# Matmuls of the convolution taps, the stick-breaking scores and the state-space outputs contract over 128 partitions instead of 64; the taps' strided operand becomes contiguous

## Chip, cores and metric

One core of one Trainium2 chip. The metric is the device time of one execution, in microseconds, median of three runs.

## The reference

Two blocks of two layers each run over 1024 tokens of width 1024. The first block has a pooling and attention layer and a Hyena layer; the second has a state-space (S5) layer and a stick-breaking attention layer, each followed by a gated feed-forward net. Three places matter here:

```
# Hyena filters: hidden units (64 wide, two sine layers) times w3, 1024 positions
h = (hdn @ w3).reshape(L, HY_ORDER, 2, HY_WIDTH) * decay

# S5 output: states (64 per group) times C, plus a local term and the skip
y = einsum('lbgp,ghp->blgh', s_re, c_re) - einsum('lbgp,ghp->blgh', s_im, c_im) + d_skip * x

# stick-breaking attention, 16 heads of 64
z = einsum('bhqd,bhkd->bhqk', q, k) * 64 ** -0.5
weights = exp(log_sigmoid(z) + (reverse cumulative sum of log_sigmoid(-z)))    # masked to the past
```

## The kernel before, in words

Activations stand transposed (channels on the 128 partitions, tokens along the row). Most products split both operands into a high and a low part of float32r and add three matmuls (`mm3`, lines 202 to 204). Side work is written as generators that `Work.go` advances by a rate per matmul step, so that its instructions stand between the steps of the big products; a tile scheduler then fixes each engine's order. SBUF tiles of 4 KB a partition come from one pool of 40 buffers (`t`, `tr`).

**Taps** (`hy_filters`, `hy_prep`, `hy_spectrum`). The filter taps of 8 x 128 positions are products of the hidden units `hs` with panels of `w3`. `hs` holds the high part of the 64 hidden units on partitions 0 to 63 and the low part on 64 to 127. Line 896 multiplies all 128 rows with `w3h` (its 64 rows stand there twice); line 897 multiplies rows 0 to 63 with `w3l`. The stationary operand is `hsr[:, n + i]`: 128 columns that lie 8 elements apart. There are 12 spectra of 16 such matmuls. Two spectra run in the first 100 us, among the loads of the modulation weights; ten are spread over the products of `ev_in`.

**S5 outputs** (`s5_load`, `outputs` in `s5_main`). Channels come in 8 batches. Of a batch, `s5_load` reads the tables E, ph, D and Co and `u_tile` reads U (eight loads), all on SP's queue. `outputs` computes 8 groups: line 1519 is a 128-row matmul with D; lines 1520 and 1521 contract the real and imaginary states of one group over its 64 partitions (0 to 63 for even groups, 64 to 127 for odd ones). They are plain float32, so the trace shows each as two matmuls.

**Scores** (`sb_q`, `sb_k`, `sb_weights`). For each of 8 pairs of heads, copies on POOL's DMA queue make `q2` (the high part of the queries, on both halves of the partitions) and `k2` (high part of the keys on one half, low part on the other). Line 1926 multiplies them over 128 rows, line 1928 adds the mask, and line 1931 adds low queries times high keys over the 64 rows of the head, `ql[own]` and `k2[e][own]`. A tile of 128 queries has one or two such matmuls, for up to 1024 keys. ScalarE's two sigmoids, a scan on VectorE (line 1940) and a product (line 1942) give the weights, which are transposed (line 1961) and multiplied with the values (lines 1983, 1984). `sb_mix` runs 64 units (pair, head, a quarter of the queries); the scores of the next unit, and the queries, keys and values of the next pair, stand between the products of the current one.

Of the kernel before, what the change touches and what calls it, by code (L numbers as in the profile page):

```python
# [19 lines left out]
P = 128  # L20
# [24 lines left out]
class Work:  # L45
    """instructions that are issued between others, `rate` steps behind each step of a product"""
# [15 lines left out]
class Norm:  # L62
    """layer norm to a (hi, lo) tile per half, and to DRAM; st: the tiles and their sums, set by their product;
    keep: the float32 result replaces the tiles"""
# [39 lines left out]
class Core:  # L104
# [27 lines left out]
    def with_work(self, gen, fg, rate):  # L132
        """runs fg with gen between its products, then the rest of gen"""
        w = Work(gen, rate)
        self.work.insert(0, w)
        fg()
        w.drain()
        self.work.remove(w)

    def lagged(self, tasks):  # L140
        """(product, use) pairs: each use is issued behind the next product"""
# [33 lines left out]
    def weights(self, src, shape, big=False):  # L175
        """a panel of weights as (hi, lo) tiles"""
# [11 lines left out]
    def first4(self, srcs, acts):  # L188
        """four panels, the first half of all before the second; acts: tiles and columns of each half"""
# [55 lines left out]
    def rms_half(self, xs, acc, hv, gain, shift, outs, n=HB):  # L245
        """generator"""
# [19 lines left out]
    def modulation0(self):  # L266
        """shift and scale of block 0, for both conditions"""
# [31 lines left out]
    def mod_cols(self, src, th, b0, out):  # L299
        """1024 columns of a modulation, for the first condition"""  # L300
# [31 lines left out]
    def halves(hs):  # L332
        """tiles and columns of each half of the tokens"""
# [371 lines left out]
    def out_proj(self, wsrc, acts, evac, order=None, first_half=None, res=None):  # L705
        """first_half: Work, issued along with the second half of the tokens; res: tiles and what they start with"""
# [38 lines left out]
    def hy_filters(self):  # L745
        """hidden units of the filters, [64, L]; the halves of L share the partitions until the end"""
# [35 lines left out]
        hl = self.tr("hsl", (P, 2, HB))  # L782
        self.split(src, hl[:, 0], hl[:, 1])
        hs = self.tr("hs", (P, 2, HB))
        for i in range(2):
            for part in range(2):
                nc.gpsimd.dma_start(hs[64 * part:64 * part + 64, i].bitcast(F32),
                                    hl[64 * i:64 * i + 64, part].bitcast(F32))
        self.hs2 = hs.rearrange("p a b -> p (a b)")
# [7 lines left out]
    def cpair(self, out, a, b, sg):  # L797
        """out[0] = a + sg i b, out[1] = a - sg i b"""
# [7 lines left out]
    def dft8(self, x, sg, sl):  # L806
        """8 point transform of complex [4, 2, 128] tiles, in the orders of T2"""
# [43 lines left out]
    def hy_prep(self):  # L851
# [7 lines left out]
        def load(g):  # L859
# [4 lines left out]
            nc.gpsimd.dma_start(w3[0][64:].bitcast(F32), w3[0][:64].bitcast(F32))  # L864
# [17 lines left out]
    def hy_spectrum(self, g, o, ct, w3, dec, skip):  # L882
# [4 lines left out]
        hsr = self.hs2.rearrange("p (a b) -> p b a", b=8)  # L887
# [4 lines left out]
        def taps(n):  # L892
            pb = self.psb("pf")
            for i in range(2):
                ob = pb[:, i * CTX:(i + 1) * CTX]
                mm(ob, hsr[:, n + i], w3[0][:, cs], start=True, stop=False)
                mm(ob, hsr[:64, n + i], w3[1][:64, cs], start=False, stop=True)
# [60 lines left out]
    def modulation1(self):  # L958
        """gate of block 0, shift and scale of block 1, gate of block 1"""
# [21 lines left out]
    def hy_natural(self, c, part, c0):  # L981
        """a panel behind its short convolution, in a frame of 128 positions per partition"""
# [32 lines left out]
    def hy_conv(self, c, y):  # L1015
# [9 lines left out]
        for o in range(2):  # L1025
# [5 lines left out]
            def sums(neg):  # L1031
                """sums (differences) of the transforms of m and m + 4: two in PSUM, two in SBUF"""
# [432 lines left out]
    def s5_load(self, b):  # L1465
        ts = self.s5t[b] = {}
        for n, sh, src in (("E", (P, 8, 2, 64), self.e_d[b]), ("ph", (P, 2, 4, P), self.p_d[b]),
                           ("D", (P, 8, P), self.m_d[b]), ("Co", (P, 2, 4, P), self.c_d[b])):
            ts[n] = self.t("s5" + n, sh)
            self.nc.sync.dma_start(ts[n], src)  # L1470

    def u_tile(self, b):
        """a batch of channels of the S5 layer, eight tokens on the partitions"""
# [6 lines left out]
    def s5_main(self):  # L1480
# [28 lines left out]
        def outputs(b):  # L1509
# [3 lines left out]
            for hb in range(2):  # L1513
                py = self.psb("py5")
                for j in range(4):
                    g = 2 * j + hb
                    o = py[:, j * P:(j + 1) * P]
                    r = slice(hb * 64, hb * 64 + 64)
                    nc.tensor.matmul(o, Dm[:, g], U[:, g], start=True, stop=False)
                    nc.tensor.matmul(o, Co[r, 0, j], S[r, 0, j], start=False, stop=False)  # L1520
                    nc.tensor.matmul(o, Co[r, 1, j], S[r, 1, j], start=False, stop=True)
# [21 lines left out]
        def glu(b):  # L1543
            """the first two panels of the next product grow with the tiles"""
# [81 lines left out]
    def mix_out(self, wsrc, acts, res_d, norm, perm=False):  # L1626
        """out projection + ALPHA * residual (in DRAM), with the sums that the norm needs"""
# [584 lines left out]
```

## Time and profile before

| what | value |
|---|---|
| median of three runs | 4174.78 us (4172.21 to 4179.71) |
| profiled execution, first to last instruction | 4172.6 us |
| busy: PE, VectorE, ScalarE, POOL | 95%, 68%, 35%, 6% |
| granted TensorE clock, mean | 0.964 of full speed |
| chain that ended last | PE 81%, DVE 9%, issue 4%, ACT 3%, DMA 2% |

PE is TensorE's matmuls and PEld its weight loads, which may run beside matmuls. A matmul's listed duration includes its way through the array, so consecutive matmuls overlap; what a matmul costs is the distance between its start and the next start. The page gives no time for the profiled execution besides its span, which is 2.2 us under the median of the runs; what lies around the span is taken to be the same before and after.

### The profile page before, as it was taken

The page shows a single profiled execution, that of the slowest core. Times are in us where ns is not written, and L with a number is a line of the kernel's source. Part 1 is how long each engine was busy: PE and PEld are TensorE (multiplying, and loading weights), DVE is VectorE, ACT ScalarE, POOL GpSimd, SP SyncE. Part 2 cuts the span into 40 slices and gives each one's busy share as a digit, 9 for nine tenths or more (in the row PEclk, how much of TensorE's full clock was granted, in tenths as well). Part 3 has the DMA queues.
Part 4 walks back from the last instruction along what each step waited for, and adds up shares of the span by engine and source line. Part 5 has one row for each costly group of instructions (what it writes and reads, how often), then busy time and mean ns, then how long its engine had stood idle before and what let it go on. Part 6 is the DMA issues. An engine that isn't in the chain of part 4 may idle for free.

```text
span 4172.6 us, 51168 instructions
## 1 busy us (share of the span) xinstructions
PE 3949.0 (95%) x19684; PEld 3206.1 (77%) x19684; DVE 2844.1 (68%) x4892; ACT 1446.3 (35%) x2328; POOL 270.2 (6%) x482
## 2 busy tenths in 40 slices
PE   6899989999999997999999999989999899999997
PEld 3787878777888866787788888768778677888886
DVE  4666667777788968776866664367777867666544
ACT  2222225543121121333433233245555544332332
POOL 0000100022001011000000000010000000000000
PEclk9899999999999998999999999989999899999998
DMA  5333321144122247513322244322222232222542
GB/s 201 107 120 122 116 87 41 36 165 165 66 73 85 74 143 245 174 61 97 131 76 76 91 149 167 108 82 76 61 62 72 75 121 106 76 91 76 174 153 102
DMA packets 169978, 449.16 MB, mean 108 GB/s; under 512 B 37854, under 2 KB 58340, under 8 KB 169734
## 3 DMA queue, kind: packets, MB, share of 16 engines
q1 hardware_dynamic: 129126, 317.94, 23.0%
q0 software_dynamic: 38304, 123.24, 8.5%
q10 hardware_dynamic: 2304, 4.72, 0.4%
q8 instruction: 155, 2.54, 0.2%
q14 instruction: 89, 0.73, 0.1%
HBM read 327.07 MB, written 100.66 MB: 103 GB/s over the span
## 4 chain that ended last, share of the span: by engine, by line
PE 81%; DVE 9%; issue 4%; ACT 3%; DMA 2%; POOL 0%; SPq 0%; ACTq 0%; DVEq 0%; POOLq 0%
PE p L202 7%; PE p L204 7%; PE p L203 7%; PE pd L202 4%; PE pd L204 4%; PE pd L203 4%; PE pout L202 2%; PE pout L204 2%; PE pout L203 2%; DVE sbm L1940 2%; PE pu L202 2%; PE pu L204 2%; PE pu L203 2%; PE pwt L1961 1%; PE pz L1041 1%
## 5 line engine op out<-in xcount | busy, mean ns | idle before, releaser
L185 DVE TENSOR_TENSOR wl<-wt,wh 128x1024 fp32r<-128x1024 f32 x232 | 283.1, 1221 | 335.7 <-ACT wh L184 332.0
L184 ACT CAST wh<-wt 128x1024 fp32r<-128x1024 f32 x232 | 243.0, 1048 | 761.7 <-PE pd L203 213.5
L202 PE MATMUL p<-tq,wq 128*128 128x512 f32 x736 | 292.3, 397 | 3.6 <-ACT wq L215 3.6
L204 PE MATMUL p<-tq,wq 128*128 128x512 f32 x736 | 292.0, 397 | 0.0
L203 PE MATMUL p<-tq,wq 128*128 128x512 f32 x736 | 291.6, 396 | 0.0
L202 PE MATMUL pd<-hd,wh 128*128 128x512 f32 x704 | 278.9, 396 | 0.0
L204 PE MATMUL pd<-hd,wl 128*128 128x512 f32 x704 | 278.7, 396 | 0.0
L203 PE MATMUL pd<-hd,wh 128*128 128x512 f32 x704 | 278.6, 396 | 0.0
L204 PE MATMUL p<-hq,wq 128*128 128x512 f32 x480 | 190.0, 396 | 0.0
L203 PE MATMUL p<-hq,wq 128*128 128x512 f32 x480 | 189.9, 396 | 0.0
L202 PE MATMUL p<-hq,wq 128*128 128x512 f32 x480 | 189.7, 395 | 0.0
L215 ACT CAST wq<-ws 128x512 fp32r<-128x512 f32 x184 | 114.3, 622 | 211.5 <-PE p L204 206.6
L1711 DVE TENSOR_TENSOR fsg<-fsg,p 128x512 f32<-128x512 f32 x140 | 94.3, 686 | 120.1 <-PE p L204 119.9
L202 PEld LDWEIGHTS p<-tq,wq 128*128 128x128 f32 x736 | 138.9, 189 | 43.7 <-ACT wq L215 4.9
L204 PEld LDWEIGHTS p<-tq,wq 128*128 128x128 f32 x736 | 138.8, 189 | 32.4
L203 PEld LDWEIGHTS p<-tq,wq 128*128 128x128 f32 x736 | 139.2, 189 | 31.4
L1711 DVE TENSOR_TENSOR fsu<-fsu,p 128x512 f32<-128x512 f32 x140 | 94.5, 687 | 95.4 <-PE p L204 95.3
L216 DVE TENSOR_TENSOR wq<-ws,wq 128x512 fp32r<-128x512 f32 x184 | 126.6, 689 | 46.8 <-ACT wq L215 44.7
L204 PEld LDWEIGHTS pd<-hd,wl 128*128 128x128 f32 x704 | 132.5, 188 | 31.8
L203 PEld LDWEIGHTS pd<-hd,wh 128*128 128x128 f32 x704 | 132.5, 188 | 31.8
L202 PEld LDWEIGHTS pd<-hd,wh 128*128 128x128 f32 x704 | 132.4, 188 | 31.7
L202 PE MATMUL pu<-hq,wh 128*128 128x512 f32 x320 | 130.0, 406 | 9.4 <-DVE cv L978 9.4
(699 smaller groups left out, 10749.8 us busy)
## 6 DMA issues: line engine op xcount, KB each, us to landing
wt<-w_gu SPq DMA_DIRECT2D x88, 512.0 KB
wt<-w_dn SPq DMA_DIRECT2D x88, 512.0 KB
wm<-w_mod SPq DMA_DIRECT2D x48, 512.0 KB
hid<-fsg POOLq DMA_DIRECT2D x44, 512.0 KB, 4.0
hr<-hid SPq DMA_DIRECT2D x44, 512.0 KB
wt<-w_od SPq DMA_DIRECT2D x28, 512.0 KB
khat<-fX POOLq DMA_DIRECT2D x24, 512.0 KB, 3.0
kh<-khat SPq DMA_DIRECT2D x24, 512.0 KB
```

Source lines behind the costliest of these rows:

```text
L184: nc.scalar.copy(wh, wt)
L185: nc.vector.tensor_tensor(wl, wt, wh.bitcast(F32), op=ALU.subtract)
L202: mm(ps, lh, rh, start=first, stop=False)
L203: mm(ps, lh, rl, start=False, stop=False)
L204: mm(ps, ll, rh, start=False, stop=last)
L215: self.nc.scalar.copy(h, src)
L216: self.nc.vector.tensor_tensor(l, src, h.bitcast(F32), op=ALU.subtract)
L1041: mm(p4[:, i, q], tb[:, m], z[:, self.POS[m]], start=True, stop=False)
L1711: add = lambda o, u, v: tt(o, u, v, op=ALU.add)
L1940: nc.vector.tensor_tensor_scan(om[:, :n - 1], om[:, :n - 1], self.inv[:, 3:4].to_broadcast([P, n - 1]), 1.0, op0=ALU.mult, op1=ALU.add)
L1961: nc.tensor.transpose(pt[:, s * P:(s + 1) * P], W[x][:, c:c + P], self.ident)
```

## The change

`hs8` stores the hidden units in the order in which the taps read them, so that the 128 columns of a load lie next to each other; the copies that build it write rows of 64 elements. `w3l` is copied to partitions 64 to 127 as `w3h` was, and line 897 contracts over 128. In S5, Co comes as two tiles per batch, each with one half loaded and the other set to zero by POOL, and both state products contract over 128 rows. For the scores, four more copies per pair make `l2`, the low queries on both halves, and the matmul contracts over 128 rows of `l2` and `k2`. (The docstrings that the diff also removes change nothing.)

```
@@ hy_filters
-        hl = self.tr("hsl", (P, 2, HB))
-        self.split(src, hl[:, 0], hl[:, 1])
-        hs = self.tr("hs", (P, 2, HB))
+        hl = self.tr("hsl", (P, 2, 8, 64))
+        self.split(src.rearrange("p (a b) -> p a b", b=8), *(hl[:, i].rearrange("p b a -> p a b") for i in range(2)))
+        self.hs8 = self.tr("hs", (P, 8, P))
         for i in range(2):
             for part in range(2):
-                nc.gpsimd.dma_start(hs[64 * part:64 * part + 64, i].bitcast(F32),
+                nc.gpsimd.dma_start(self.hs8[64 * part:64 * part + 64, :, 64 * i:64 * i + 64].bitcast(F32),
                                     hl[64 * i:64 * i + 64, part].bitcast(F32))
-        self.hs2 = hs.rearrange("p a b -> p (a b)")
@@ hy_prep, load
-            nc.gpsimd.dma_start(w3[0][64:].bitcast(F32), w3[0][:64].bitcast(F32))
+            for part in w3:
+                nc.gpsimd.dma_start(part[64:].bitcast(F32), part[:64].bitcast(F32))
@@ hy_spectrum
-        hsr = self.hs2.rearrange("p (a b) -> p b a", b=8)
+        hsr = self.hs8
                 mm(ob, hsr[:, n + i], w3[0][:, cs], start=True, stop=False)
-                mm(ob, hsr[:64, n + i], w3[1][:64, cs], start=False, stop=True)
+                mm(ob, hsr[:, n + i], w3[1][:, cs], start=False, stop=True)
@@ s5_load
-                           ("D", (P, 8, P), self.m_d[b]), ("Co", (P, 2, 4, P), self.c_d[b])):
+                           ("D", (P, 8, P), self.m_d[b])):
+        ts["Co"] = []
+        for hb in range(2):
+            own, oth = slice(64 * hb, 64 * hb + 64), slice(64 - 64 * hb, P - 64 * hb)
+            co = self.t("s5Co", (P, 2, 4, P))
+            self.nc.gpsimd.memset(co[oth], 0.0)
+            self.nc.sync.dma_start(co[own], self.c_d[b][own])
+            ts["Co"].append(co)
@@ s5_main, outputs
-                    nc.tensor.matmul(o, Co[r, 0, j], S[r, 0, j], start=False, stop=False)
-                    nc.tensor.matmul(o, Co[r, 1, j], S[r, 1, j], start=False, stop=True)
+                    nc.tensor.matmul(o, Co[hb][:, 0, j], S[:, 0, j], start=False, stop=False)
+                    nc.tensor.matmul(o, Co[hb][:, 1, j], S[:, 1, j], start=False, stop=True)
@@ sb_q
+        q2, l2 = ([self.tr(n) for _ in range(2)] for n in ("q2", "l2"))
                 nc.gpsimd.dma_start(q2[e][r].bitcast(F32), qh[own].bitcast(F32))
+                nc.gpsimd.dma_start(l2[e][r].bitcast(F32), ql[own].bitcast(F32))
-        yield q2, ql
+        yield q2, l2
@@ sb_weights
-                nc.tensor.matmul(ps[:, c0:c1], ql[own, qc], k2[e][own, ks], start=False, stop=True)
+                nc.tensor.matmul(ps[:, c0:c1], l2[e][:, qc], k2[e][:, ks], start=False, stop=True)
```

On PE the order stays as it was but for the first taps and for the first score tile of the second head of a pair, in seven of the eight pairs. There the scores (`psz`) stood behind the products with the values of the unit before (`pso`). PE before:

```order
L204 MATMUL psg<-hq,wl 128x512
L1983 MATMUL pso<-wT,sbv 128x256
L1984 MATMUL pso<-wT,sbv 128x256
L1983 MATMUL pso<-wT,sbv 128x128
L1984 MATMUL pso<-wT,sbv 128x128
L1926 MATMUL psz<-k_20864,q_20848 128x512
L1928 MATMUL psz<-sbmask,identr 128x128
L1926 MATMUL psz<-k_20864,q_20848 128x512
L1931 MATMUL psz<-k_20864,sql 128x512 x2
```

PE with the change (the same lines are six numbers higher):

```order
L204 MATMUL psg<-hq,wl 128x512
L1932 MATMUL psz<-k_20905,q_20883 128x512
L1934 MATMUL psz<-sbmask,identr 128x128
L1932 MATMUL psz<-k_20905,q_20883 128x512
L1989 MATMUL pso<-wT,sbv 128x256
L1937 MATMUL psz<-k_20905,l_20885 128x512 x2
L1932 MATMUL psz<-k_20905,q_20883 128x512
L1990 MATMUL pso<-wT,sbv 128x256
L1989 MATMUL pso<-wT,sbv 128x256
L1990 MATMUL pso<-wT,sbv 128x256
```

The scores now stand ahead of eight value products, six of 256 columns and two of 128.

POOL's queue issues the copies of a pair's queries (`q`, high part; `l`, low part) and keys (`k`). Of the first pair, before:

```order
L1871 DMA q_20847<-sqh 64x1024 x2
L1871 DMA q_20848<-sqh 64x1024 x2
L1883 DMA k_20863<-skh 64x1024
L1884 DMA k_20863<-skl 64x1024
L1883 DMA k_20864<-skh 64x1024
L1884 DMA k_20864<-skl 64x1024
```

With the change:

```order
L1877 DMA q_20882<-sqh 64x1024
L1878 DMA l_20884<-sql 64x1024
L1877 DMA q_20882<-sqh 64x1024
L1878 DMA l_20884<-sql 64x1024
L1877 DMA q_20883<-sqh 64x1024
L1878 DMA l_20885<-sql 64x1024
L1877 DMA q_20883<-sqh 64x1024
L1878 DMA l_20885<-sql 64x1024
L1890 DMA k_20904<-skh 64x1024
L1891 DMA k_20904<-skl 64x1024
L1890 DMA k_20905<-skh 64x1024
L1891 DMA k_20905<-skl 64x1024
```

The keys' copies have four more copies ahead of them.

## Rows read from the trace of the kernel before

**Rows 1.** The page's first line.

```profile
span 4172.6 us, 51168 instructions
```

**Rows 2.** Busy time by stretch: length, busy of PE to POOL, clock, DMA share, GB/s.

```profile
107.00:530.00 423.00, 407.94 (x1994) 329.41 (x1994) 261.74 (x481) 97.41 (x133) 35.02 (x49) 0.94 0.34 116
1640.00:1730.00 90.00, 82.21 (x546) 64.87 (x542) 70.75 (x142) 18.00 (x22) 4.00 (x12) 0.87 0.83 259
2860.00:3290.00 430.00, 411.99 (x2375) 337.98 (x2373) 340.43 (x435) 233.78 (x434) 27.73 (x54) 0.98 0.24 66
3290.00:3345.00 55.00, 44.35 (x207) 33.74 (x208) 46.74 (x63) 29.86 (x60) 1.09 (x2) 0.77 0.24 83
```

**Rows 3.** Timeline of PE at one group of four taps: start, us, what.

```profile
223.05 0.28 PE L896 MATMUL pf<-w3h,hs 128*128 128x256 f32 x1
223.27 0.51 PE L897 MATMUL pf<-w3l,hs 64*128 64x256 f32 x1
...
224.59 0.50 PE L202 MATMUL pbg<-hh,wh 128*128 128x512 f32 x1
```

**Rows 4.** The chain, in order of time: start, time to the next start, what.

```profile
41.29 0.54 PE pf L896
...
62.41 0.22 PE pk L947 x2
...
2889.90 0.23 PE psg L203
...
2912.56 0.12 PE psv L204
```

**Rows 5.** Weight loads of the taps: ns min/median/max, first and last start.

```profile
L896 PEld LDWEIGHTS pf<-w3h,hs x96: 312/315/335, 36.9 to 526.0; 128*128 128x128 f32 x96
```

**Rows 6.** Weight loads of the scores, the same columns.

```profile
L1926 PEld LDWEIGHTS psz<-k,q x192: 186/189/338, 2787.7 to 3333.4; 128*128 128x128 f32 x192
...
L1931 PEld LDWEIGHTS psz<-k,sql x192: 182/183/335, 2789.1 to 3334.1; 64*128 64x128 f32 x192
```

**Rows 7.** Timeline of PE at one score tile.

```profile
2900.86 0.39 PE L1926 MATMUL psz<-k,q 128*128 128x384 f32 x1
2901.17 0.66 PE L1931 MATMUL psz<-k,sql 64*128 64x512 f32 x2
2901.77 0.50 PE L202 MATMUL psg<-hq,wh 128*128 128x512 f32 x1
2902.11 0.40 PE L203 MATMUL psg<-hq,wh 128*128 128x512 f32 x1
```

**Rows 8.** PE's waits, 2787 to 3345: us in total, times, longest.

```profile
PE pwt L1961 <- DVE sbb L1942: 13.7, 22, 1.6
...
PE psz L1926 <- DMA k<-skl: 5.8, 1, 5.8
```

**Rows 9.** The chain at the first unit of a second head.

```profile
2897.45 0.66 PE psz L1931 x2
...
2906.93 0.30 PE pwt L1961
```

**Rows 10.** Timeline of POOL, copies of the first pair's queries.

```profile
2778.92 2.08 POOL L1871 DMA_DIRECT2D q<-sqh  x4 [26.45 <-ACT sqh L1864]
```

**Rows 11.** Timeline of PE, one group of S5 outputs at full clock, one at half.

```profile
1718.64 0.49 PE L1519 MATMUL py<-s5U,s5D 128*128 128x128 f32 x2
...
1719.70 0.49 PE L1519 MATMUL py<-s5U,s5D 128*128 128x128 f32 x2
...
1757.41 0.79 PE L1519 MATMUL py<-s5U,s5D 128*128 128x128 f32 x2
...
1759.28 0.80 PE L1519 MATMUL py<-s5U,s5D 128*128 128x128 f32 x2
```

**Rows 12.** Timeline of SP, loads of the last batch, and the first matmul on them.

```profile
1719.15 9.26 SPq L1478 DMA_DIRECT2D s5U<-xf_d  x8
...
1730.96 1.09 PE L1492 MATMUL pe_re<-s5U,s5E 128*64 128x128 f32 x16 [1.88 <-DMA s5yt<-s5y]
```

More of the change, by code (lines that the diff above doesn't have):

```diff
@@ L1517, in outputs @@
                     o = py[:, j * P:(j + 1) * P]
-                    r = slice(hb * 64, hb * 64 + 64)
                     nc.tensor.matmul(o, Dm[:, g], U[:, g], start=True, stop=False)
-                    nc.tensor.matmul(o, Co[r, 0, j], S[r, 0, j], start=False, stop=False)
-                    nc.tensor.matmul(o, Co[r, 1, j], S[r, 1, j], start=False, stop=True)
+                    nc.tensor.matmul(o, Co[hb][:, 0, j], S[:, 0, j], start=False, stop=False)
+                    nc.tensor.matmul(o, Co[hb][:, 1, j], S[:, 1, j], start=False, stop=True)
                 nc.scalar.copy(Y[:, hb::2], py.rearrange("p (g c) -> p g c", g=4))
@@ L1861, in sb_q @@
         qh, ql = self.tr("sqh"), self.tr("sql")
-        q2 = [self.tr("q2") for _ in range(2)]
+        q2, l2 = ([self.tr(n) for _ in range(2)] for n in ("q2", "l2"))
         for hv, pq in zip(HALVES, halves):
@@ L1916, in sb_weights @@
         nc = self.nc
-        q2, ql, k2 = qk
-        own = slice(64 * e, 64 * e + 64)
+        q2, l2, k2 = qk
         for qt in (2 * j, 2 * j + 1):
```

## The prediction

> **What bounds the kernel now.** I read the page first (a span of 4172.6 us [rows 1], PE busy for 95% of it), then the stretches in which the three edited matmuls run, and in each of them the starts of matmuls, not their listed durations. In the stretch of the taps PE is busy 407.9 of 423 us; in that of the scores 412.0 of 430, with VectorE busy 340.4 of the same 430; in that of the S5 outputs 82.2 of 90, and there the DMA engines are 83% busy, at 259 GB/s [rows 2]. So PE is the bound in the first two, with VectorE not far behind in the second, and in the third DMA is beside it.
>
> The reader is to see one thing in the starts: a matmul that contracts over 64 rows costs time around it. Of four taps in a row the first takes 0.22 us to the next start, and all four 1.54 us [rows 3], although 256 columns over 128 rows cost 0.12 us elsewhere [rows 4]. In a score tile, 384 columns ahead of the 64-row matmuls take 0.31 us to the next start, where 512 columns over 128 rows take 0.23 [rows 4] and 384 hence 0.17; the two 64-row matmuls of 512 and 384 columns take 0.60 us, where 0.40 is due; the first matmul behind them takes 0.34 instead of 0.23 [rows 7].
>
> **The taps.** 192 matmuls, 48 groups of four. A group takes 1.54 us [rows 3], and I take it to make the next matmul 0.10 us longer, as the scores do (0.34 for 0.23) [rows 7]; at 0.12 us each it would take 0.48 [rows 4]. Saved: 1.16 us. Two things go, the change of row count and the strided load (315 ns [rows 5] against 189 for a contiguous one [rows 6]); I need not part them, since both go.
> - Eight groups lie in the first 100 us. The first 16 matmuls cost 0.54 us each, at half clock [rows 4]; at twice 0.12 they cost 0.24, which saves 4.8 us. The second 16 I count at 4.5 us. PE runs on from there without a wait, so both shorten the path.
> - 40 groups lie in the stretch up to 530 us: 46 us. PE idles 15 us of 423 there [rows 2]. Time saved ahead of such a wait only makes the wait longer, and VectorE's and ScalarE's part of the taps is not shortened, so I take nine tenths: 41 us.
> - Against it: the copies that build `hs8` write pieces of 256 B where 2 KB stood, and `w3l` needs a copy behind `w3h`'s, for which PE waits before its first taps. Bounds: nothing, if they land within that wait, and 5.8 us, the wait for such a copy that a row shows [rows 8], if a whole landing is added. I take 2, nearer to nothing, because the copy of `w3l` follows at once and the first four matmuls now need `w3h` alone.
>
> Sum of the taps: 4.8 + 4.5 + 41 - 2 = **48 us**.
>
> **The scores.** There are 128 tiles, 64 with two 64-row matmuls and 64 with one. A tile with two loses 0.14 + 0.20 + 0.11 = 0.45 us [rows 7]; one with one I put at 0.35 (the same without the second matmul's 0.10). That is 51 us of PE time. Not all of it is on the path:
> - The last pair has no other work to fill PE. PE is busy 44.4 us of 55 and VectorE 46.7 [rows 2], so its 16 tiles give nothing.
> - Twice in a pair the path runs through VectorE: behind the first scores of a head, 1024 keys wide, two scans and their products take until the transposes, from 2897.45 to 2906.93, 9.5 us [rows 9]. Two tiles lie inside each, 28 in seven pairs. They give nothing.
> - The transposes wait 22 times for VectorE already [rows 8]; I take one tile's gain from each.
> - The other 62 tiles give 0.40 us each: 25 us.
> - In seven units the first scores stand ahead of eight value products. That starts VectorE's chain by 6 x 0.12 + 2 x 0.06 = 0.85 us earlier, 6 us in all; bounds 0 and 6, I take 3, since the last of the chain also waits for those products.
> - Four more copies stand ahead of the first keys on POOL. Four cost 2.08 us to issue [rows 10], and PE waits 5.8 us for these keys [rows 8]: 2 us more, once. For later pairs the copies are issued under the products of the pair before; the queue was idle ahead of them (26.5 us for the first [rows 10]).
>
> Sum of the scores: 25 + 3 - 2 = **26 us**.
>
> **The S5 outputs.** A group of six matmuls takes 1.06 us at full clock and 1.87 at half [rows 11]. Float32 matmuls of the same size over 128 rows take 0.22 us a pair [rows 4], so 0.67 a group, 1.33 at half clock. Of 64 groups about 17 are at half clock: 47 x 0.39 + 17 x 0.54 = 28 us of PE time. But SP's queue issues loads without a break up to the last U, whose eight loads take 9.3 us to issue and end at 1728.4; the last batch's first matmul follows at 1730.96, after a wait of 1.9 us [rows 12]. The DMA engines are 83% busy up to there [rows 2]. So what the first six batches save turns into a wait for that load. The outputs of the seventh batch save 3 us and then wait for VectorE; those of the eighth, 8 groups at half clock, save 8 x 0.54 = 4.3. One more load per batch on SP, some 0.4 us, is six ahead of the last U: up to 2.4 us lost. The clearing of the other halves runs on POOL, which is busy 4 us of 90 [rows 2], beside all this. Bounds -3 and 28; I take **4 us**, near the low end, because the load's end stands in a row.
>
> **Sum.** 48 + 26 + 4 = 78 us. Against the profiled span that is 4094.6; the median of the runs is 2.2 us above the span, so 4174.8 - 78 = **4097 us**.
>
> **A rule that speaks against the change.** Loads of 64 and of 128 rows last 183 and 189 ns [rows 6], so the number of rows does not change the load. The Trainium skill ("TensorE: Matmul & The Clock Gate", "LDWEIGHTS (loading the stationary operand)") says that a load's time goes by its columns and not by the contraction. The durations agree with it. Taken alone it would leave nothing to gain from 128 rows. By that the sum would be the third rival's; by the starts [rows 3, 7], which place the loss between the matmuls and not in the load itself, it is the one above.
>
> **Rivals.**
> 1. *All PE time is on the path.* 55 us of taps (46 for 41, no cost at the start), 51 of scores and 28 of S5: 134, hence 4041 us. For it: PE is busy 95%. Against it: the VectorE chain [rows 9] and the last U [rows 12]. Chance 0.06.
> 2. *VectorE takes up the scores.* It is busy 79% of the stretch [rows 2]; if its chain binds in most units, the scores give 5, and S5 nothing, and the taps 38 because more waits show: 43, hence 4132. Chance 0.12.
> 3. *The row count does not matter* and only the stride did: 192 x (315 - 189) ns [rows 5, 6] = 24 us, hence 4151. Against it: the scores' loads are not strided and still lose 0.45 us a tile [rows 7]. Chance 0.04.
> 4. *The copies of the low queries hold the keys back: slower.* The pool of 40 tiles has to give two more per pair. If `l2` gets the buffer of a tile that the current pair reads until its end, POOL waits there with the key copies behind it. PE would then stand at each of seven pair starts for twelve copies (6.2 us), a landing (5.8 [rows 8]) and about half of VectorE's chain (4 [rows 9]): 16 us, 112 in all. With the scores' 26 gone as well, 52 - 112 gives 4235. It decides at about 7 us per pair (52 us). Against it: POOL waited for the queries themselves [rows 10], not for a buffer. Chance 0.03.
>
> **How the numbers follow.** The forecast has 0.75, with bounds of its own from 4065 (scores 40, taps 52, S5 18) to 4120. The range from 4056 to 4135 adds the second rival and leaves out the first, the third, the fourth and some of the tails. About 0.2% (8 us) is what a measurement of this kernel can tell from no change. Faster by more than that: all cases but the fourth, 0.96; within it 0.01; slower 0.03.
>
> **What would show it.** In the profile after, four taps should take about 0.5 us and their loads 190 ns; the lines of the scores should follow each other at 0.23 us per 512 columns, and a group of S5 outputs should take 0.67 us. The stretch of the taps should end some 50 us earlier; that of the scores should be 25 us shorter, with more waits of the transposes for VectorE; S5 should end at most 10 us earlier against its start, with PE waiting for U. The forecast is wrong if four taps still take over 1 us (rival 3), if the stretch of the scores keeps its length (rival 2), or if PE waits for keys or low queries in later pairs (rival 4).

## Result, and the profile after

| | before | after |
|---|---|---|
| median of the runs, us | 4174.83 | 4099.04 (4097.87 to 4101.86) |
| profiled execution: time and span, us | span [rows 1] | 4098.59, span 4096.8 |
| ratio to before | | 0.9817, 95% interval 0.9803 to 0.9831 |
| PE busy in the span | 95% | 93% |

The kernel is 76 us faster; forecast were 78. Measured again beside the experiment on the keys' copies, the same kernel is about 70 us faster, at a ratio of 0.9832 (0.9815 to 0.9849); the two intervals overlap. To see where the time went, the starts of the same matmuls are set against each other in the two profiled executions:

| first or last start of | before, us | after, us | after minus before |
|---|---|---|---|
| first tap | 37.0 | 35.8 | -1.1 |
| first product behind the first filters (`pbg`) | 107.0 | 92.7 | -14.3 |
| last tap | 526.4 | 468.5 | -57.9 |
| first state product of S5 (`pe_re`) | 1639.4 | 1585.3 | -54.1 |
| last output of S5 (`py`) | 1762.7 | 1703.0 | -59.6 |
| first product of the attention's values (`psv`) | 2752.9 | 2694.1 | -58.8 |
| first score | 2787.7 | 2734.2 | -53.5 |
| last score | 3334.1 | 3255.7 | -78.4 |
| last matmul | 4156.4 | 4081.6 | -74.8 |

In this pair of profiles the taps gave about 58 us, S5 5.6, the scores 24.9 from the first to the last; the first score lost 5.3 of its lead. Nearly 4 us each were given back between the taps and S5 and behind the scores. Both stretches show a lower granted clock after (a mean of 0.96 for 0.97, and 0.98 for 0.99), and ahead of S5 PE waits 12.7 us for the first tile U, where it waited 10.6. So 2.1 us of the first loss belong to the S5 part of the change.

One profile is not exact to a few us, mainly because the granted clock differs from run to run. The kernels of the experiments below leave some parts as they were and change others, so each stretch can be read several times:

| stretch, us | part as before | part changed | difference of the means |
|---|---|---|---|
| first to last tap | 487.7 to 496.3 (5 kernels) | 429.4 to 433.4 (7) | 61 |
| S5, first state product to last output | 123.3 to 125.9 (5) | 114.8 to 122.8 (5) | 7 |
| first to last score | 542.5 to 546.4 (6) | 521.5 to 523.5 (5) | 22 |

The last row leaves out the kernels without the scan and the one with another order of copies in every pair; the second leaves out those without S5's loads.

The stretches of [rows 2], in the kernel after (columns as there); the fourth row is the whole stretch of the scores, and below it stands the same of before.

```profile
93.00:472.00 379.00, 357.71 (x1994) 299.92 (x1994) 260.87 (x481) 96.28 (x133) 36.30 (x51) 0.95 0.39 131
1586.00:1680.00 94.00, 68.38 (x565) 61.30 (x564) 74.39 (x148) 17.58 (x22) 14.93 (x24) 0.84 0.85 251
2808.00:3223.00 415.00, 379.88 (x2378) 330.73 (x2379) 340.90 (x435) 234.69 (x435) 40.44 (x79) 0.99 0.31 82
2734.20:3255.70 521.50, 471.36 (x2923) 409.46 (x2924) 428.94 (x545) 295.31 (x549) 46.52 (x91) 0.97 0.31 83
```

```profile
2787.70:3334.10 546.40, 518.99 (x2923) 423.75 (x2923) 431.58 (x545) 294.99 (x549) 32.36 (x63) 0.94 0.24 66
```

The taps' stretch has the same 1994 matmuls and is 44 us shorter, while PE's time in it fell by 50. In S5 PE is busy 68 of 94 us, where it was busy 82 of 90: PE now waits. In the scores PE's time fell by 47.6 us and the stretch by 24.9, with VectorE's time nearly unchanged, so the other 22.7 us became idle time of PE. A part of both falls is the clock's: its mean over the stretch was 0.94 and is 0.97.

PE's timeline at four taps, to be held against [rows 3]:

```profile
202.19 0.28 PE L896 MATMUL pf<-w3h,hs 128*128 128x256 f32 x1
202.31 0.28 PE L897 MATMUL pf<-w3l,hs 128*128 128x256 f32 x1
202.43 0.28 PE L896 MATMUL pf<-w3h,hs 128*128 128x256 f32 x1
202.55 0.28 PE L897 MATMUL pf<-w3l,hs 128*128 128x256 f32 x1
202.66 0.40 PE L202 MATMUL pbg<-hh,wh 128*128 128x512 f32 x1
202.90 0.40 PE L203 MATMUL pbg<-hl,wh 128*128 128x512 f32 x1
```

The four starts stand 0.12 us apart, the group takes 0.47 us where it took 1.54, and the product behind it 0.24. PE's timeline at one score tile, of the shape of [rows 7]:

```profile
2841.82 0.39 PE L1932 MATMUL psz<-k,q 128*128 128x384 f32 x1
2842.05 0.57 PE L1937 MATMUL psz<-k,l 128*128 128x512 f32 x2
2842.45 0.40 PE L202 MATMUL psg<-hq,wh 128*128 128x512 f32 x1
2842.69 0.40 PE L203 MATMUL psg<-hq,wh 128*128 128x512 f32 x1
```

Its steps are 0.23, 0.40 and 0.24 us, where they were 0.31, 0.60 and 0.34: 0.38 us less. PE's waits in the stretch of the scores, after (columns of [rows 8]):

```profile
PE pwt L1967 <- DVE sbb L1948: 27.6, 24, 2.8
PE pso L1990 <- DVE wT L216: 13.3, 25, 1.0
PE psz L1932 <- DMA k<-skh: 11.1, 1, 11.1
PE pso L1989 <- ACT wT L215: 7.3, 16, 0.6
```

The transposes wait for VectorE twice as long as before (27.6 us for 13.7 [rows 8]), and the wait for the first keys has doubled, from 5.8 to 11.1. In S5 PE's waits before (1634 to 1770 us) and after are:

```profile
PE pe_re L1492 <- DMA s5U<-xf_d: 10.6, 1, 10.6
PE py L1520 <- DVE s5S L1243: 7.6, 2, 5.1
PE pe_re L1492 <- DMA s5yt<-s5y: 1.9, 1, 1.9
```

```profile
PE pe_re L1499 <- DMA s5U<-xf_d: 18.0, 3, 12.7
PE py L1526 <- DVE s5S L1243: 9.3, 3, 5.1
PE pe_re L1499 <- DMA s5yt<-s5y: 8.0, 3, 5.1
```

The longest wait of each first row (10.6 and 12.7) is for the first U and lies ahead of the first state product, outside the stretch. Inside it the state products wait five times, 13.4 us in all (5.4 by the row of U and 8.0 by that of `s5yt`, the load of the transposed outputs), where they waited once, for 1.9 us. A state product does not read `s5yt`, which is loaded on the same queue, so I read these waits as waits for U: the products that wait for 1.9 us before and for 5.1 after start 2.6 and 2.7 us after the last load of their U has been issued. A group of S5 outputs takes 0.67 us at full clock (1663.97 to 1664.64), for 1.06 [rows 11].

### The profile page after: what moved, and what is told of

Same layout as the page of the kernel before. It is cut to its first block, busy times and chain, and to the rows that moved or that the text cites. A ratio compares the mean times of both kernels' runs of the same rounds, so it can differ in the third digit from the quotient of the medians.

```text
span 4096.8 us, 51285 instructions
## 1 busy us (share of the span) xinstructions
PE 3816.4 (93%) x19684; PEld 3148.8 (77%) x19684; DVE 2842.5 (69%) x4892; ACT 1446.9 (35%) x2328; POOL 304.0 (7%) x533
## 4 chain that ended last, share of the span: by engine, by line
PE 72%; DVE 11%; issue 4%; ACT 3%; DMA 2%; POOL 1%; SPq 1%; DVEq 0%; ACTq 0%; POOLq 0%
PE p L202 7%; PE p L203 7%; PE p L204 7%; PE pd L202 4%; PE pd L203 4%; PE pd L204 4%; PE pout L202 2%; PE pout L204 2%; PE pout L203 2%; PE pu L202 2%; PE pu L204 2%; PE pu L203 2%; DVE sbm L1946 2%; PE pwt L1967 1%; PE pz L1041 1%
```

## Experiments

**The three parts one by one.** Theory: the parts touch different stretches and add up, and each gives what the starts show. The rivals stand in the expectations. Each kernel is the one before with one part of the diff.

The taps alone (`hy_filters`, `load` and `hy_spectrum` of the diff):

```diff
-        hs = self.tr("hs", (P, 2, HB))
+        self.hs8 = self.tr("hs", (P, 8, P))
...
-                mm(ob, hsr[:64, n + i], w3[1][:64, cs], start=False, stop=True)
+                mm(ob, hsr[:, n + i], w3[1][:, cs], start=False, stop=True)
```

> Only the taps part of the change, on the kernel before: contiguous stationary tiles, and both halves of the taps' weights copied so that all four matmuls contract over 128 rows. By the prediction's terms: 48 us less (4.8 + 4.5 + 41 - 2). By the theory from the two traces (the first matmuls and the modulation matmuls behind them reach the full clock earlier, and the copies cost no start): 56 to 59 us less, the first product behind the filters' first units some 14 us earlier, and no part of the gain given back up to the S5 layer. The rival (the taps give 48 and the rest of the measured 76 comes from shifted clock stretches elsewhere): 46 to 50 us less.

Measured: 4118.61 us, ratio 0.9854 (0.9837 to 0.9871), so 61 us less by the ratio (54 to 68). The last tap starts 59.6 us earlier, the first `pbg` 11.9. That is the theory's figure and not 48. By the profile 3 us were given back up to the first state product of S5, and another 2 to the end of S5, which the theory had put at nothing; that stretch, which this kernel does not change, took 125.8 us here for 123.3, as it did in three other kernels with S5 as before (125.8, 125.9 and 125.9), and the granted clock had been higher in the 123.3 (a mean of 0.85, for 0.78 here).

The scores alone (`sb_q` and `sb_weights`):

```diff
+                nc.gpsimd.dma_start(l2[e][r].bitcast(F32), ql[own].bitcast(F32))
...
-                nc.tensor.matmul(ps[:, c0:c1], ql[own, qc], k2[e][own, ks], start=False, stop=True)
+                nc.tensor.matmul(ps[:, c0:c1], l2[e][:, qc], k2[e][:, ks], start=False, stop=True)
```

> Only the scores part: copies of the low queries on both halves of the partitions, second product of the scores over 128 rows. By the prediction's terms: 26 us less. By the theory from the two traces: the first scores start 5 us later (the keys' copies stand behind four more copies and share the queue with them), the stretch from the first to the last score is 25 us shorter, 19 to 20 us less in all. By the rival that VectorE takes up the scores: 5 us less.

Measured: 4155.39 us, ratio 0.994 (0.9925 to 0.9955): 25 us less (19 to 31). From the first to the last score 521.7 us for 546.4: 24.7 less, as in the whole change. From the first `psv` to the first score it takes 40.3 us for 34.8: 5.5 lost. The rival that VectorE takes up the scores is out.

The S5 part alone (`s5_load` and `outputs`):

```diff
+            self.nc.gpsimd.memset(co[oth], 0.0)
+            self.nc.sync.dma_start(co[own], self.c_d[b][own])
...
-                    nc.tensor.matmul(o, Co[r, 0, j], S[r, 0, j], start=False, stop=False)
+                    nc.tensor.matmul(o, Co[hb][:, 0, j], S[:, 0, j], start=False, stop=False)
```

> Only the S5 part: two zero-filled tables per batch, outputs over 128 rows. By the prediction's term and by the traces: 4 to 7 us less from the first state product to the last output, since the loads of U end when they did. If PE time set the end of this stretch: 28 us less. If the additional load per batch and the clearing cost more than the outputs gain: up to 3 us more.

Measured: 4172.02 us, ratio 0.999 (0.9979 to 1.0001), which is 4 us and hardly told from nothing. In the profile the stretch from the first state product to the last output takes 117.7 us for 123.3, 5.6 less, as in the whole change; ahead of it PE waits 12.5 us for the first U, for 10.6, so some 4 us are left. 28 is out, and so is a loss of 3.

The three ratios sum to 2.16% less time (give or take 0.25 by their intervals), the whole change to 1.83% (0.14). The parts account for the whole; if anything the whole gives a little less than their sum.

**Stride and row count of the taps.** The change removes two things from the taps at once, which the prediction did not part. One kernel takes the contiguous tiles and keeps the low half of the weights on 64 rows; the other takes 128 rows everywhere and keeps the strided tile.

```diff
-        hsr = self.hs2.rearrange("p (a b) -> p b a", b=8)
+        hsr = self.hs8
```

> Taps with contiguous stationary tiles, but the low half of the weights still over 64 rows. If only the stride mattered (third rival): a group of four takes about 0.5 us, as in the kernel after, and the gain is that of the whole taps part, 50 to 58 us. If the change of row count costs by itself: at 0.12 us a matmul and, as in the scores of the kernel before, 0.25 us more for each 64-row matmul, a group takes about 1.0 us and the gain is about 26 us.

```diff
-            nc.gpsimd.dma_start(w3[0][64:].bitcast(F32), w3[0][:64].bitcast(F32))
+            for part in w3:
+                nc.gpsimd.dma_start(part[64:].bitcast(F32), part[:64].bitcast(F32))
...
-                mm(ob, hsr[:64, n + i], w3[1][:64, cs], start=False, stop=True)
+                mm(ob, hsr[:, n + i], w3[1][:, cs], start=False, stop=True)
```

> Taps over 128 rows in all four matmuls, but from the strided tile. If only the stride mattered: a group stays near 1.5 us, gain within 3 us of nothing. If only the row count mattered: about 0.5 us, 50 to 58 us less. If each costs by itself: the strided loads, 0.126 us longer than contiguous ones, set the pace at about 0.25 us a matmul, a group takes about 1.0 us, gain about 26 us.

Measured: 4155.03 us (ratio 0.9936, 0.9921 to 0.995) for the contiguous tiles alone, 4136.65 us (0.9893, 0.9876 to 0.9909) for the rows alone: 27 and 45 us less. PE's timeline at four taps, contiguous with 64 rows:

```profile
210.75 0.28 PE L895 MATMUL pf<-w3h,hs 128*128 128x256 f32 x1
210.96 0.38 PE L896 MATMUL pf<-w3l,hs 64*128 64x256 f32 x1
211.27 0.38 PE L895 MATMUL pf<-w3h,hs 128*128 128x256 f32 x1
211.58 0.38 PE L896 MATMUL pf<-w3l,hs 64*128 64x256 f32 x1
211.89 0.50 PE L202 MATMUL pbg<-hh,wh 128*128 128x512 f32 x1
```

And strided with 128 rows:

```profile
207.35 0.29 PE L897 MATMUL pf<-w3h,hs 128*128 128x256 f32 x1
207.47 0.41 PE L898 MATMUL pf<-w3l,hs 128*128 128x256 f32 x1
207.72 0.41 PE L897 MATMUL pf<-w3h,hs 128*128 128x256 f32 x1
207.96 0.41 PE L898 MATMUL pf<-w3l,hs 128*128 128x256 f32 x1
208.21 0.39 PE L202 MATMUL pbg<-hh,wh 128*128 128x512 f32 x1
```

Medians over the groups at full clock:

| | strided | contiguous |
|---|---|---|
| 64 rows in the second matmul | 1.54 us, next product 0.34 | 1.15 us, next product 0.34 |
| 128 rows in all | 0.86 us, next product 0.23 | 0.47 us, next product 0.23 |

The stride costs 0.39 us a group in either row, the row count 0.68 in either column and 0.10 at the product behind. The two costs add. (By the times they come to 27 + 45 us for the 61 of both, which the intervals allow.) With alternating row counts the steps behind the first are 0.31 us, with equal row counts 0.24 (strided) or 0.12; so at contiguous tiles a step among alternating row counts costs 0.19 us more, in either direction. The expectation of 26 us held in time for the stride, though the group was told as 1.0 us and takes 1.15. For the rows it was too low: I had put 0.25 us on each 64-row matmul, and its two changes cost 0.38.

**What took up the rest of PE's time.** Two pairs of kernels leave out work of another engine, before and after the change alike. In the first pair the loads of S5 are replaced by clearing on GpSimd and the scores have no scan:

```diff
+            if b < 2 or n == "Co":
+                self.nc.sync.dma_start(ts[n], src)
+            else:
+                self.nc.gpsimd.memset(ts[n], 0.0)
...
-            nc.vector.tensor_tensor_scan(om[:, :n - 1], om[:, :n - 1], self.inv[:, 3:4].to_broadcast([P, n - 1]), 1.0,
-                                         op0=ALU.mult, op1=ALU.add)
```

> The kernel before with two loads taken off. In the S5 layer the tables E, ph and D and the tile U of batches 2 to 7 are cleared on GpSimd instead of loaded; in the scores the scan is left out, so the weights are the product of the two sigmoids. This is the partner of the next run: the difference between the two, stretch by stretch, is the gain of the change when DMA does not pin S5 and VectorE has two thirds of its work in the scores. Its own stretches should be shorter than in the kernel before: S5 by 5 to 15 us, the scores by 10 to 40 us.

> The changed kernel with the same parts left out (tables and U of batches 2 to 7 cleared instead of loaded, no scan in the scores). Against the run before it: if loads pinned S5, its gain there grows from 5 us to 10 to 28 us (28 is all PE time saved; VectorE, 72 us busy, may be next); if something else did, it stays at 4 to 7. If VectorE's chain took up the part of the scores' 51 us that did not show (25 did, inside the stretch), the gain from the first to the last score grows to 40 to 51 us; if the PE time was wrongly worked out, it stays near 25.

Measured: 4120.43 and 4038.51 us, one run each. The scores, first to last, in the two kernels (busy time by stretch; the kernel before first):

```profile
2783.90:3283.10 499.20, 495.39 (x2936) 411.32 (x2936) 272.36 (x424) 294.71 (x552) 32.37 (x63) 0.98 0.27 73
```

```profile
2734.20:3198.60 464.40, 455.93 (x2937) 401.77 (x2937) 271.47 (x423) 294.75 (x552) 46.39 (x91) 1.00 0.35 94
```

Without the scan PE's time falls by 39.5 us and the stretch by 34.8: nine tenths show, where with the scan half did (24.9 of 47.6). The granted clock differs between these four stretches, so I set against each other the time from the first score of the fourth pair of heads to that of the fifth, at the full clock in all four kernels: before and after with the scan, then before and after without it.

```profile
3004.07:3076.30 72.23, 68.46 (x410) 56.60 (x409) 56.51 (x73) 38.57 (x74) 4.62 (x9) 1.00 0.23 65
2939.77:3008.94 69.17, 63.55 (x410) 55.81 (x409) 56.14 (x73) 38.78 (x74) 6.66 (x13) 1.00 0.31 84
2986.60:3054.13 67.53, 67.22 (x409) 56.59 (x409) 36.07 (x57) 38.55 (x74) 4.63 (x9) 1.00 0.26 70
2920.01:2983.24 63.23, 62.61 (x410) 55.82 (x409) 36.08 (x57) 38.70 (x74) 6.63 (x13) 1.00 0.37 93
```

With the scan 3.1 us show of 4.9 that PE saves, without it 4.3 of 4.6. So VectorE's chain had taken up most of what did not show. The gain stays below the 40 to 51 that I expected, because PE has less to save than I had worked out (below). The first kernel's own stretch of the scores is 47 us shorter than in the kernel before, more than the 10 to 40 told.

For S5 this pair tells nothing: the gain there was 4.7 us, but in the second kernel PE waited 17.9 us behind GpSimd's clearing, the work that I had put in for the loads:

```profile
PE pe_re L1505 <- POOL s5S L1516: 17.9, 6, 3.4
PE pe_re L1505 <- DMA s5U<-xf_d: 12.7, 1, 12.7
```

The second pair has neither loads nor clearing; batches 2 to 7 use the tiles of batches 0 and 1:

```diff
+        if b >= 2:
+            self.s5t[b] = dict(self.s5keep[b % 2])
+            return
         ts = self.s5t[b] = {}
```

> The kernel before, with the tables and the tile U of batches 2 to 7 not loaded and not cleared: batches 0 and 1 are used again for all (so the S5 layer's output is another). Partner of the next run. Its stretch from the first state product to the last output was 123.3 us; 100 to 118 without those loads.

> The changed kernel with the same loads left out. If the loads pin the S5 layer, its gain over the run before it, from the first state product to the last output, is 10 to 28 us in place of the 5.6 between the two kernels as they are. If VectorE's chain (74 of 92 us busy there) or the first U, for which PE waits 12.7 us, sets the stretch: 4 to 7 us as before.

Measured, one run each: 4176.74 and 4080.51 us. S5 from the first state product to the last output (busy time by stretch; the kernel before first):

```profile
1649.00:1762.30 113.30, 106.32 (x689) 83.23 (x689) 88.67 (x175) 26.31 (x31) 4.54 (x13) 0.85 0.27 91
```

```profile
1585.40:1680.90 95.50, 81.86 (x688) 74.36 (x689) 88.18 (x175) 26.27 (x31) 4.52 (x13) 0.89 0.32 108
```

The stretch is 17.8 us shorter, where with the loads it was 5.6, at nearly the same fall of PE's time (24.5 us here, 22.7 there: 111.3 to 88.6). PE's waits tell the same: in this pair no state product inside the stretch waits for a load, where 13.4 us of such waits stood in the changed kernel. So the loads did pin S5 and took most of these 12 us of the gain; a part of the 12 can be the clock's, whose mean went from 0.85 to 0.89 in this pair. With the loads gone VectorE, busy 88 of 95.5 us, is probably next.

**The keys' copies.** Theory: the first keys come 5 us later because they stand behind eight copies in place of four on GpSimd's queue. A kernel issues, for each head, the high queries, the keys and then the low queries:

```diff
@@ sb_q
-                nc.gpsimd.dma_start(q2[e][r].bitcast(F32), qh[own].bitcast(F32))
-                nc.gpsimd.dma_start(l2[e][r].bitcast(F32), ql[own].bitcast(F32))
+                self.late += [lambda e=e, r=r, own=own: nc.gpsimd.dma_start(q2[e][r].bitcast(F32), qh[own].bitcast(F32)),
+                              lambda e=e, r=r, own=own: nc.gpsimd.dma_start(l2[e][r].bitcast(F32), ql[own].bitcast(F32))]
@@ sb_k
+            a, b, c, f = self.late[4 * e:4 * e + 4]
+            a(), c()
             nc.gpsimd.dma_start(k2[e][own].bitcast(F32), kh[own].bitcast(F32))
             nc.gpsimd.dma_start(k2[e][oth].bitcast(F32), kl[own].bitcast(F32))
+            b(), f()
```

> The changed kernel with its copies on GpSimd's queue in another order: for each head the high queries, then the keys, then the low queries, in place of all queries of both heads ahead of the keys. If the keys of the first pair came late because they stood behind eight copies and shared the DMA engines with them: PE's wait ahead of the first scores falls from 11 us to 5 to 7, and the time falls by 4 to 6 us against the changed kernel. If the keys' own landing (8 us) sets it whatever stands ahead: within 2 us of the changed kernel.

> The changed kernel itself, on the same chip as the run before it, so that the two can be compared: 4097 to 4101 us.

Measured: 4136.51 us (ratio to before 0.99, 0.9884 to 0.9916) against 4108.53 for the changed kernel (0.9832, 0.9815 to 0.9849). The repeat of the changed kernel lies above the 4097 to 4101 told. The wait for the keys fell further than told, to 4.5 us, but the kernel is 28 us slower than the changed one: a miss. From the first to the last score it takes 563.7 us for 523.2. From the first scores of one pair to those of the next the changed kernel takes 69.2 us in the five intervals between the second and the seventh pair, this one 71.6 to 80.4. ScalarE (ACT in the rows) and VectorE wait there, between 2790 and 3260 us, for copies that the changed kernel's rows do not name; VectorE's row:

```profile
DVE wT L216 <- DMA k<-skl: 21.1, 4, 7.0
```

POOL's longest wait ahead of a copy of the queries, in this kernel and in the changed one:

```profile
POOL q L1877 <- PE pwt L1971: 80.6, 3, 26.9
```

```profile
POOL q L1877 <- ACT sqh L1870: 103.6, 6, 17.3
```

The changed kernel's POOL waits for the queries themselves (`sqh`), this one's for transposes (`pwt`).

In the later pairs the copies run beside the current pair and all tiles come from one pool. My reading is that a copy of the queries that is issued only after the keys are there keeps its source tile occupied longer; POOL then waits until the transposes have read the buffer that `q2` is given, and VectorE and ScalarE wait, to write `wT`, for a copy of the keys that stands behind it. This would be the mechanism of the prediction's fourth rival, in a kernel that brings it about. Next the other order was taken for the first pair alone, where nothing runs beside it:

```diff
+                cq = lambda e=e, r=r, own=own: nc.gpsimd.dma_start(q2[e][r].bitcast(F32), qh[own].bitcast(F32))
+                cl = lambda e=e, r=r, own=own: nc.gpsimd.dma_start(l2[e][r].bitcast(F32), ql[own].bitcast(F32))
+                if self.late is not None:
+                    self.late += [cq, cl]
+                else:
+                    cq(), cl()
...
+        self.late = None
```

> The changed kernel with the other order of copies for the first pair alone, where no other work runs beside them; the seven later pairs keep their order. If the run with the order changed in all pairs lost its time because in the later pairs the delayed copies held buffers that VectorE and ScalarE wanted (their waits for the copies of the keys, 33 us, stand in its trace): later pairs take 69.2 us again, PE's wait ahead of the first scores stays at 4 to 6 us in place of 11, and the time is 5 to 7 us below the changed kernel, about 4092 to 4103. If the order itself slows the scores: the later pairs still take over 71 us each and the time is above 4110.

Measured: 4091.76 us (4089.85 to 4098.61), ratio 0.9798 (0.9777 to 0.982). The five later intervals take 69.2 us again. PE's wait ahead of the first scores:

```profile
PE psz L1942 <- DMA k<-skl: 4.4, 1, 4.4
```

From the first `psv` to the first score it takes 33.5 us, for 40.2 in the changed kernel and 34.8 before. So the order of the first pair's copies cost the changed kernel these 6.7 us, and the loss of the run before came from the order in the later pairs, where copies run beside other work. That buffers carry this loss is read from its waits; the later pairs keep their order in this run, so it does not part buffers from order. By its median this kernel is 7 us under the changed one as first measured and 17 under its repeat, but the intervals of the ratios overlap: that the first scores come earlier is shown by the profile, that the kernel is faster is not shown by the times.

## Why the prediction was right

The time came within 2 us of the forecast and the mechanism was the one forecast. That it came so near is partly luck: two terms were off by 10 and 6 us in opposite directions, the repeat of the kernel gave 70 us in place of 76, and the stretches move by a few us between profiles.

- **Taps: 48 forecast, 58 measured.** The first 32 matmuls were put at 4.8 + 4.5 us; they gave 3.4 (8.5 us from the first tap to the first modulation matmul behind, now 5.1) and 5.3 (9.3 with four modulation matmuls between, now 4.0). The two dozen modulation matmuls behind each sixteen, which had no term, gave 1.9 (12.3, now 10.4) and 2.1 (12.5, now 10.4) more. Of the second two dozen the profile shows why: PE's granted clock in that stretch was a mean of 0.83 before and is 1.00 now, the higher of its two levels, 2.4 GHz. The rows (before, then after):

```profile
79.30:91.80 12.50, 12.50 (x25) 2.15 (x24) 3.25 (x6) 1.86 (x4) 0.00 (x0) 0.83 0.10 42
```

```profile
67.50:77.90 10.40, 10.40 (x25) 1.96 (x24) 8.51 (x19) 2.40 (x4) 1.11 (x2) 1.00 0.25 101
```

  What stood ahead of them was sixteen taps, alternating 64 and 128 rows before, 128 rows alone after. For the first two dozen the clock's records begin too late to give a mean (at 49.4 us before, 41.0 after, both at the higher level), but the steps of the matmuls show the level: before, the first four modulation matmuls follow each other at 0.81 to 0.85 us and, from 49.6 us on, at 0.43; after, all of them at 0.43 to 0.45 from 40.9 us on. So before they began at half the pace, and this is the 1.9 us. With contiguous tiles and 64 rows the records begin at 47.8, with strided tiles and 128 rows at 42.9. That goes with the row count, and I leave it at that.
- **The start cost: 2 forecast, 0.8 measured**, which lies inside the 3.4. The copy of `w3l` shows as a wait of 0.6 us before the first low matmul, whose step is 0.97 us where the others take 0.21. The first tap starts 1.1 us earlier, but over all runs it starts between 35.3 and 37.8 us whatever the kernel, so the pieces of 256 B show nowhere.
- **The 40 groups: 41 forecast, 43.6 measured** (57.9 - 14.3). A group saves 1.07 + 0.10 us, as told (1.16); nine tenths of it on the path was nearly right. The granted clock, whose mean over these stretches differs (0.94 and 0.95), has a part in the 43.6.
- **Scores: 26 forecast, 19.6 measured** in the profile (24.9 from the first to the last, less 5.3 at their start; by the means over several kernels 22, less 5.4). Here two errors of opposite sign lie inside the 25 us term. PE's time was put at 51 us. The 47.6 by which it fell in this pair of profiles hold a difference of the granted clock; at the full clock it falls by 4.9 us a pair of heads, which makes 39 in eight. I had taken 0.17 us as due for 384 columns ahead of the low queries [rows 7], and the same step takes 0.23 over 128 rows, so a tile with two saves 0.38 and not 0.45; a tile with one saves 0.34, as told (0.35). That makes 46, and why PE saves less than that is not shown. And half of it was taken to show, by counting tiles; at the full clock 3.1 of 4.9 do, by way of more and longer waits of the transposes and the value products, not tile by tile. The 3 us for the moved score tiles can't be seen apart from it. The last pair, put at nothing, is part of the last stretch and gave about 2.
- **The keys' copies: 2 forecast, 5.3 measured.** This is the term that failed. I priced the issue of four more copies [rows 10] and not their transfers: the copies of the first pair now move 3.15 MB in place of 2.1 over the same queue, and PE waits 11.1 us for 5.8. The copy of the first head's low keys is issued 2.5 us later after the first copy of queries (5.1 for 2.7), and takes 8.8 us from issue to landing for 6.0; the first score starts 0.2 us behind its landing after and 0.1 before.
- **S5: 4 forecast, 5.6 measured** in the stretch, less the 2.1 by which the first U comes later; the prediction had put up to 2.4 on the additional loads. It is pinned by the loads as told, with PE waiting for U; without them 17.8 would show.

The rivals: all PE time on the path would have given 4041, and S5 and the scores show why not. VectorE does take up the scores, but a part of them, not all. The third rival, that row count does not matter, falls by two kernels: rows alone gave 45 us, contiguous tiles alone 27. The fourth did not happen in the changed kernel; when the copies are issued later, waits of its kind appear. The Trainium skill's sentence that a weight load's time goes by its columns ("TensorE: Matmul & The Clock Gate", "LDWEIGHTS (loading the stationary operand)") agrees with the durations here (183 ns for 64 rows in the contiguous kernel, 188 for 128) and says nothing of what decided: the longer step between matmuls of unequal row count, and the strided source.

## What to carry to other kernels

Read the cost of a matmul from the starts of it and of its neighbours, not from its duration: here the steps around a matmul over half the rows cost more than those around one over all of them, because the row count changed on both sides of it, and padding the contraction with zeros, or with a second copy of the operand, was the cheaper form. Before counting saved PE time as time, look at which load or which engine ends the wait next; about four tenths of the scores' (at the full clock) and three quarters of S5's went there. When copies are added to a queue, count what they move and not only their issue. Issuing first what is waited for first brought the first scores forward by 6.7 us where nothing ran beside the copies, and lost 28 us where other work did. And before a difference of a few us between two profiles is given to a change, hold their granted clocks against each other: here that is worth several us in each stretch.

## What the runs showed that I had not expected

- A change between 64 and 128 rows in successive matmuls costs about 0.2 us at contiguous tiles, in both directions: 0.10 at the step in which the count changes and 0.10 at the next one. It is so in all three places. In the taps each step within a group is a change and also follows one, and takes 0.31 us for 0.12; the first step (0.21 for 0.12) and the product behind the group (0.34 for 0.23) have one part each. A group with its four changes costs 0.78 us more. In a score tile with two low products four steps in a row take 0.09 to 0.10 more each, also the one from a 64-row matmul of 512 columns to another 64-row one (0.34 for 0.23), which follows a change; two changes, 0.38 in all. In S5 there are two changes and 0.39 us a group.
- The S5 groups show that it is the change that costs and not the 64 rows. Line 1519 has 128 rows, 1520 and 1521 have 64; two such matmuls take 0.22 us in the changed kernel. Before:

```profile
1718.64 0.49 PE L1519 MATMUL py<-s5U,s5D 128*128 128x128 f32 x2
1719.06 0.49 PE L1520 MATMUL py<-s5S,s5Co 64*128 64x128 f32 x2
1719.39 0.38 PE L1521 MATMUL py<-s5S,s5Co 64*128 64x128 f32 x2
```

  The six steps of such a group are, at the median, 0.21, 0.21, 0.21, 0.11, 0.11 and 0.20 us, where all six are 0.11 with 128 rows. The second of the six is the change to 64 rows and the last the change back; the first and the third each follow a change. The two steps that neither hold a change nor follow one, between 64-row matmuls, run at the full pace. An order of the matmuls with fewer changes would then gain too; no run tries it.
- A stationary tile read at a stride of eight elements sets a pace of 0.24 us a matmul of 256 columns for 0.12, and this adds to the cost of the row change instead of hiding under it.
- Issuing copies of the queries later in every pair, with the same work in them, cost 28 us (4136.51 for 4108.53); the waits point at held buffers.
